# A hybrid block on one core: SSD decay taken off GpSimd, TensorE in program order there, and four smaller edits

## The chip, the cores and the metric

The kernel runs on one core of one Trainium2 chip. A core has five engines with an instruction queue each: TensorE (PE in the profile, PEld its weight loads), VectorE (DVE), ScalarE (ACT), GpSimd (POOL) and SyncE (SP), which here only issues DMAs. The metric is the time of one launch in microseconds; lower is better. Before the change it is 2102.24 us, the median of three runs from 2101.9 to 2103.63 us.

## The reference, cut to what matters

One layer on 256 tokens of width 2048, all in float32. The projection `w_in` of the normalised input feeds a stick-breaking attention, a Mamba-2 scan (SSD) and two gates; both mixers are merged, projected, normed and added to x; a gated MLP of width 5632 with a width-3 convolution follows, again normed and added. The part that the change touches most is the SSD, per group g of 8 heads (8 groups, head width 64, state 128), after a width-4 causal convolution and SiLU:

```
la = dt * a;  cs = cumsum(la)                       # falls along the tokens
decay = exp(where(causal, cs[l] - cs[s], -inf))     # per head, l >= s
cb    = C @ B^T                                     # per group
y     = (cb * decay) @ (x * dt)  +  carried state  +  x * d_skip
y     = rms_norm(y * silu(z), per group) 
```

## The kernel before, in words

**Weights.** All matrices stream from memory in 714 units of 128x1024 float32 (512 KB). SP issues the loads (L78). Each unit is split into a rounded half `whi` (a cast on ACT, L63) and a remainder `wlo` (a subtraction on DVE, L64). Five buffers of each exist and units are split three ahead of use, so the cast of unit n+5 waits until TensorE has finished unit n. `feat_mm` gives a tile of 128 features by 256 tokens (16 k-steps of a 512-column product, L112, and a 256-column one, L113); `tok_mm` gives two tiles of 128 tokens by 512 features (L145 to L147, three products per tile and k-step). Their banks are four of the eight PSUM banks; the pool `paux` has the other four.

**Background work.** Small products are put between the large ones by generators in a list `bg`; `pump()` advances the oldest by one `yield`, and `drain()` runs the list empty. `tok_mm` pumps after every fourth k-step, that is after every two units. Outside of a few hand-ordered places (`manual_schedule`) the framework's scheduler fixes each engine's order before the run, by its own priorities, close to program order; each queue then runs strictly in that order.

**Group loop.** A group does four `ps_xs` tiles, two `ps_bc` tiles (convolution on DVE, `cva`, and SiLU on ACT, L318), then `ps_z`. During `ps_z` and the next group's `ps_xs`, `ssd_work` (L323 to L380) runs in steps: transposes `px` of the convolved x (L332) with the scaled copies `xw` and `xd`; the decay matrix `mm` (csb minus cs_tok on DVE, L338; masked on GpSimd by `affine_select`, L339; exponential on ACT, L347; times `pcb` on DVE, L350); `pcb`, the C-by-B product (L343, L344), one pump after `px`; `po`, the carried-state product (L353), one pump later; `pd`, the decay product (L363), in two pumps; then gate, norm and the transposes `pt` (L385). `csb` is a broadcast of cs from a DRAM copy (L429).

**Around it.** At the start, ten pairs of products on `ones` keep TensorE busy (`wake`) while x chunk 0 and the first weights land. Between the mixers' output product `ps_mo` and the MLP's first tiles `ps_f` stands the norm `n1`: the block is scaled (L632), transposed (`pth`, L385) and split into halves `h` (L63, L64). After the last product `ps_fo` come the norm `n3` and the output: a sum of squares on ACT (L571), a product with the gain (L701), three small Newton steps (L594 to L596), nine multiply-adds (L726) and nine DMAs (L727) issued in turn by ACT and SP.

Of the kernel before, what the change touches and what calls it, by code (L numbers as in the profile page):

```python
# [29 lines left out]
C_N = KT + C_FB + 88  # L30

LNEXP = "natural_log_exp_and_others"
ACT_DVE = {mybir.EngineType.Activation, mybir.EngineType.DVE}
# [5 lines left out]
def block_kernel(ctx, tc, xT, xN, wts, vecs, rows, hvec, dskip, gain, out):  # L39
# [95 lines left out]

    def tok_mm(acts, nk, name):

        pss = [mm_bank(f"{name}_{t}") for t in range(2)]
        for k in range(nk):
            if k % 2 == 0:  # L140
                hi, lo = unit()
            w = slice(k % 2 * 512, k % 2 * 512 + 512)
            for t in range(2):
                ah, al = (acts[k // 4][:, k % 4, s, t * P:(t + 1) * P] for s in range(2))
                nc.tensor.matmul(pss[t], ah, hi[:, w], start=(k == 0), stop=False)  # L145
                nc.tensor.matmul(pss[t], ah, lo[:, w], start=False, stop=False)  # L146
                nc.tensor.matmul(pss[t], al, hi[:, w], start=False, stop=(k == nk - 1))  # L147
            if k % 4 == 3:
                pump()
        return pss  # L150
# [19 lines left out]
    for i in range(10):  # L170
# [152 lines left out]
    def ssd_work(g, xf, bf, cf, xs, csb):  # L323
        h8 = slice(8 * g, 8 * g + 8)
        sz, xd = xs[:, 0], xs[:, 1]
# [3 lines left out]
        for t in range(2):  # L329
# [4 lines left out]
            nc.scalar.copy(xd[:, t, :], px)  # L334
            nc.gpsimd.tensor_tensor(v3(xd[:, t, :]), v3(xd[:, t, :]), bc_in(dsk[:, h8], 64), op=ALU.mult)
        nc.gpsimd.tensor_tensor(v3(xw[:, 2, :]), v3(xw[:, 0, :]), bc_in(dec0[:, h8], 64), op=ALU.mult)
        for t in range(2):
            nc.vector.tensor_tensor(mm[:, t, :, :], csb[:, :, t * P:(t + 1) * P], bc_in(cs_tok[:, t, h8], P), op=ALU.subtract)  # L338
# [470 lines left out]
```

## Time and profile before

| | before |
|---|---|
| runs, median (range) | 2102.24 us (2101.9 to 2103.63) |
| the profiled execution | 2101.31 us, its span 2099.6 us |
| mean granted TensorE clock | 0.995 |
| TensorE busy | 2072.1 us, 99% |
| VectorE, ScalarE, GpSimd busy | 1386.0, 1156.9, 152.3 us |
| memory traffic | 191 GB/s over the span |

The profiled execution's own time is 1.71 us more than its span. A row of the timeline gives the start, the length, the engine, the line, the operation with its result and operands, how many instructions the row joins, and in brackets the idle time before it and what ended that. Matmuls overlap: successive 512-column products start about 0.23 us apart although each is listed with 0.39 us, so distances between starts, not lengths, say how long TensorE takes.

### The profile page before, as it was taken

To read this page: it belongs to the slowest core of one execution; us is meant where nothing else is said; L and a number is where in the kernel's file an instruction comes from. 1 tells how busy PE (TensorE), PEld (TensorE's weight loads), DVE (VectorE), ACT (ScalarE), POOL (GpSimd) and SP (SyncE) were. 2 spreads that over 40 slices of the span, in tenths; PEclk is the share of its full clock that TensorE was granted. 3 is DMA by queue.
4 is the path that set the end of the run, shared out by engine and by line. 5 is a ranking of instruction groups with operands and counts; after the bars stand their busy time and mean duration, and the time that the engine had idled before them with its cause. 6 is when DMAs were issued, how large, how long until landed. Compare 5 with 4: busy or idle time off the path is not lost.

```text
span 2099.6 us, 27950 instructions
## 1 busy us (share of the span) xinstructions
PE 2072.1 (99%) x10632; PEld 1760.7 (84%) x10632; DVE 1386.0 (66%) x1794; ACT 1156.9 (55%) x1542; POOL 152.3 (7%) x134
## 2 busy tenths in 40 slices
PE   9999999999999999999999999999999999999997
PEld 7788888888888888888888888788888888888886
DVE  6888877788544445555544566598878887854443
ACT  6767677667543334555556444475555555544442
POOL 0222102222000000000000021100000000000000
PEclk9999999999999999999999999999999999999999
DMA  8564565555555555555555746475555555565653
GB/s 297 194 205 160 190 205 186 176 199 179 187 197 192 192 194 186 180 171 171 170 172 185 274 161 210 141 250 191 189 190 190 189 189 190 191 232 202 195 193 109
DMA packets 109094, 402.79 MB, mean 192 GB/s; under 512 B 12416, under 2 KB 12672, under 8 KB 106656
## 3 DMA queue, kind: packets, MB, share of 16 engines
q1 hardware_dynamic: 104912, 380.07, 54.1%
q0 software_dynamic: 3328, 20.02, 2.7%
q8 instruction: 83, 1.36, 0.3%
q10 hardware_dynamic: 720, 0.93, 0.1%
q14 instruction: 51, 0.42, 0.1%
HBM read 396.71 MB, written 4.26 MB: 191 GB/s over the span
## 4 chain that ended last, share of the span: by engine, by line
PE 92%; POOL 2%; DVE 2%; issue 2%; DMA 1%; ACT 1%; SPq 0%; DVEq 0%; ACTq 0%; POOLq 0%
PE ps_fv L112 8%; PE ps_fg L112 8%; PE ps_qk L112 6%; PE ps_xs L112 5%; PE ps_fo L147 4%; PE ps_fo L145 4%; PE ps_fo L146 4%; PE ps_fg L113 4%; PE ps_fv L113 4%; PE ps_qk L113 3%; PE ps_ssd L147 3%; PE ps_ssd L145 3%; PE ps_ssd L146 3%; PE ps_xs L113 2%; PE ps_bc L112 2%; PE ps_z L146 2%
## 5 line engine op out<-in xcount | busy, mean ns | idle before, releaser
L64 DVE TENSOR_TENSOR wlo<-raw,whi 128x1024 fp32r<-128x1024 f32 (+1 forms) x715 | 905.1, 1270 | 601.2 <-ACT whi L63 600.6
L63 ACT CAST whi<-raw 128x1024 fp32r<-128x1024 f32 (+1 forms) x715 | 746.2, 1051 | 793.7 <-PE ps_fo L147 128.9
L112 PE MATMUL ps_fg<-h,whi 128*128 128x512 f32 x688 | 240.7, 394 | 0.0
L112 PE MATMUL ps_fv<-h,whi 128*128 128x512 f32 x688 | 240.6, 394 | 0.0
L113 PE MATMUL ps_fg<-h,wlo 128*128 128x256 f32 x688 | 190.6, 277 | 0.0
L113 PE MATMUL ps_fv<-h,wlo 128*128 128x256 f32 x688 | 190.6, 277 | 0.0
L112 PE MATMUL ps_qk<-a,whi 128*128 128x512 f32 x512 | 181.3, 398 | 0.0
L112 PE MATMUL ps_xs<-a,whi 128*128 128x512 f32 x464 | 162.9, 396 | 0.0
L112 PEld LDWEIGHTS ps_fv<-h,whi 128*128 128x128 f32 x688 | 129.0, 188 | 30.0
L112 PEld LDWEIGHTS ps_fg<-h,whi 128*128 128x128 f32 x688 | 129.0, 188 | 30.0
L113 PE MATMUL ps_qk<-a,wlo 128*128 128x256 f32 x512 | 143.5, 280 | 0.0
L145 PE MATMUL ps_fo<-whi,f 128*128 128x512 f32 x352 | 136.9, 389 | 0.0
L147 PE MATMUL ps_fo<-whi,f 128*128 128x512 f32 x352 | 136.9, 389 | 0.0
L146 PE MATMUL ps_fo<-wlo,f 128*128 128x512 f32 x352 | 136.9, 389 | 0.0
L113 PEld LDWEIGHTS ps_fg<-h,wlo 128*128 128x128 f32 x688 | 129.2, 188 | 0.0
L113 PEld LDWEIGHTS ps_fv<-h,wlo 128*128 128x128 f32 x688 | 129.2, 188 | 0.0
L113 PE MATMUL ps_xs<-a,wlo 128*128 128x256 f32 x464 | 129.0, 278 | 0.0
L112 PEld LDWEIGHTS ps_qk<-a,whi 128*128 128x128 f32 x512 | 96.1, 188 | 22.6
L145 PE MATMUL ps_z<-whi,a 128*128 128x512 f32 x256 | 103.7, 407 | 0.0
L112 PEld LDWEIGHTS ps_xs<-a,whi 128*128 128x128 f32 x464 | 87.1, 188 | 19.6
L146 PE MATMUL ps_z<-wlo,a 128*128 128x512 f32 x256 | 100.4, 392 | 1.0 <-DVE wlo L64 1.0
L147 PE MATMUL ps_z<-whi,a 128*128 128x512 f32 x256 | 100.1, 391 | 0.0
(282 smaller groups left out, 3832.5 us busy)
## 6 DMA issues: line engine op xcount, KB each, us to landing
raw<-wts SPq DMA_DIRECT2D x713, 512.0 KB, 3.8
csb<-cs_dram POOLq DMA_DIRECT2D x8, 1024.0 KB, 8.1
xt<-xN SPq DMA_DIRECT2D x2, 1024.0 KB, 10.6
csb<-gain POOLq DMA_DIRECT2D x8, 256.0 KB, 4.1
xn<-xN POOLq DMA_DIRECT2D x2, 1024.0 KB, 7.9
x_dram<-xn POOLq DMA_DIRECT2D x2, 1024.0 KB, 9.0
xe<-x_dram POOLq DMA_DIRECT2D x2, 1024.0 KB, 10.3
x<-xT SPq DMA_DIRECT2D x3, 512.0 KB, 9.2
```

What stands on the lines that cost most here:

```text
L63: nc.scalar.copy(hi, src)
L64: nc.vector.tensor_tensor(lo, src, hi.bitcast(F32), op=ALU.subtract)
L112: nc.tensor.matmul(ps, hi[:, w], act[:, k % 4, :, :].rearrange("p s t -> p (s t)"), start=(k == 0), stop=last)
L113: nc.tensor.matmul(ps[:, :T], lo[:, w], act[:, k % 4, 0, :], start=False, stop=last, skip_group_check=True)
L145: nc.tensor.matmul(pss[t], ah, hi[:, w], start=(k == 0), stop=False)
L146: nc.tensor.matmul(pss[t], ah, lo[:, w], start=False, stop=False)
L147: nc.tensor.matmul(pss[t], al, hi[:, w], start=False, stop=(k == nk - 1))
```

## The change

- **Decay and skip.** GpSimd loses all arithmetic of `ssd_work`. The skip product and the state-decay product go to DVE; the copy of `px` on ACT is gone, since DVE reads `px` in PSUM directly. The causal mask moves from `mm` (2048 columns, GpSimd) to `pcb` (two 128-column products with `m_le` on DVE, into `xw[:, 3]`), and the exponent is clamped by a Relu on ACT: per token tile one Relu and one Exp of 1024 columns in place of one Exp of 2048.
- **Order.** From group 1 to the end of the last group's work TensorE keeps program order. `csb`'s DMA is issued inside `ssd_work`. The `yield` between `px` and `pcb` is gone; `pd` and what follows come one pump later from group 1 on.
- **Loads.** The skip factors come with the vector load `vecs` in place of a DMA of their own. x chunk 0 is one DMA, not two halves, and `wake` has 12 pairs.
- **Small products.** `lead=True` puts one 64-column product on `ones` ahead of three tiles: `ps_qk0_0_0`, `ps_fg2`, `ps_fg3`.
- **n1.** The scalings, transposes and splits are written in another order.
- **Tail.** In the last `ps_fo` the final three units are first used for token tile 0 alone, then for tile 1; norm, scaling and output run tile by tile.

```diff
-    def feat_mm(acts, name):
+    def feat_mm(acts, name, lead=False):
         ps = mm_bank(name)
+        if lead:
+            nc.tensor.matmul(ps[:, :64], ones, ones[:, :64], start=True, stop=True)
...
+    def tok_mm_lag(acts, nk, name, lag=3):
+        pss = [mm_bank(f"{name}_{t}") for t in range(2)]
+        held = []
+        for k in range(nk):
+            left = (nk - 1 - k) // 2
+            if k % 2 == 0:
+                w = unit(min(WBUFS - 2, left) if left < lag else WBUFS - 2)
+            if left < lag:
+                held.append((k, w))
+                tok_step(pss, acts, k, nk, 0, *w)
+            else:
+                for t in range(2):
+                    tok_step(pss, acts, k, nk, t, *w)
+        for k, w in held:
+            tok_step(pss, acts, k, nk, 1, *w)
+        return pss
...
-    for i in range(10):
+    for i in range(12):
         nc.tensor.matmul(wake[:, :P], ones, ones, start=True, stop=True)
...
+    nc.sync.dma_start(x_raw[0], xT[:, 0:4, :])
     for i in range(2):
-        nc.sync.dma_start(x_raw[0][:, 2 * i:2 * i + 2, :], xT[:, 2 * i:2 * i + 2, :])
         nc.sync.dma_start(raw0[:, i * 512:i * 512 + 512], wts[0][:, i * 512:i * 512 + 512])
...
-    dsk = const.tile([P, 64], F32, name="dsk")
-    nc.gpsimd.dma_start(dsk, dskip.partition_broadcast(P))
+    dsk = vec[:, C_D:C_D + 64]
...
-    def ssd_work(g, xf, bf, cf, xs, csb):
+    def ssd_work(g, xf, bf, cf, xs):
+        csb = slot(F32, [8, T], f"csb{g}")
+        nc.gpsimd.dma_start(csb, cs_dram[h8, :].partition_broadcast(P))
+        if g > 0:
+            yield
...
-            nc.scalar.copy(xd[:, t, :], px)
-            nc.gpsimd.tensor_tensor(v3(xd[:, t, :]), v3(xd[:, t, :]), bc_in(dsk[:, h8], 64), op=ALU.mult)
-        nc.gpsimd.tensor_tensor(v3(xw[:, 2, :]), v3(xw[:, 0, :]), bc_in(dec0[:, h8], 64), op=ALU.mult)
-        for t in range(2):
-            nc.vector.tensor_tensor(mm[:, t, :, :], csb[:, :, t * P:(t + 1) * P], bc_in(cs_tok[:, t, h8], P), op=ALU.subtract)
-            nc.gpsimd.affine_select(out=mm[:, t, :, :], in_=mm[:, t, :, :], pattern=[[0, 8], [1, P]], compare_op=ALU.is_ge,
-                                    fill=-30000.0, base=0, channel_multiplier=-1)
-        yield
+            nc.vector.tensor_tensor(v3(xd[:, t, :]), v3(px), bc_in(dsk[:, h8], 64), op=ALU.mult)
         pcb = paux.tile([P, 512], F32, tag="aux", name=f"pcb{g}")
...
+        cbm = xw[:, 3, P:3 * P]
         nc.scalar.copy(xw[:, 3, 0:P], pcb[:, P:T])
+        for t in range(2):
+            nc.vector.tensor_tensor(cbm[:, t * P:(t + 1) * P], pcb[:, 256 * t:256 * t + P], m_le, op=ALU.mult)
         lnexp()
-        nc.scalar.activation(mm, mm, AF.Exp)
+        for t in range(2):
+            m = mm[:, t, :, :]
+            nc.vector.tensor_tensor(m, csb[:, :, t * P:(t + 1) * P], bc_in(cs_tok[:, t, h8], P), op=ALU.subtract)
+            nc.scalar.activation(m, m, AF.Relu, scale=-1.0)
+            nc.scalar.activation(m, m, AF.Exp, scale=-1.0)
+        nc.vector.tensor_tensor(v3(xw[:, 2, :]), v3(xw[:, 0, :]), bc_in(dec0[:, h8], 64), op=ALU.mult)
+        yield
...
-        nc.gpsimd.tensor_tensor(xd[:, 1, :], xd[:, 1, :], off, op=ALU.add)
+        nc.vector.tensor_tensor(xd[:, 1, :], xd[:, 1, :], off, op=ALU.add)
         yield
+        if g > 0:
+            yield
...
+        if g == 1:
+            order.enter_context(tc.manual_schedule(engines=PE))
...
+        for i in range(3):
+            scaled(i)
+        halves(0)
+        for i in range(3, 8):
+            halves(i - 2)
+            scaled(i)
+        halves(6)
+        halves(7)
...
-        n3.add(3, 0, ps[0])
-        n3.add(3, 1, ps[1])
-        gained(3, 0, gfo)
-        n3.last()
-        gained(3, 1, gfo)
-        n3.newton()
-        for n in range(4):
-            for t in range(2):
+        for t in range(2):
+            w = slice(t, t + 1)
+            n3.add(3, t, ps[t])
+            gained(3, t, gfo)
+            n3.last(w)
+            n3.newton(w)
+            for n in range(4):
```

How the order of the instructions moves is shown at three places. A row has the line, the operation, and result and operands; the number in a name is the tile's or the unit's, the last one a buffer's.

**Group 2, TensorE, around `px`.** First before, then with the change (`whi55` to `whi58` are weight units of `ps_z2`).

```order
L147 MATMUL ps_z2_1_1801<-whi55_1744,a0_117 128x512
L332 MATMUL px2_0_1840<-ident_203,xf2_0_1419 128x128
...
L332 MATMUL px2_1_1848<-ident_203,xf2_3_1614 128x128
L145 MATMUL ps_z2_0_1800<-whi56_1766,a1_136 128x512
...
L343 MATMUL pcb2_1901<-bc2_1_1786,bc2_0_1730 128x256
L344 MATMUL pcb2_1901<-bc2_1_1786,bc2_0_1730 128x128
L145 MATMUL ps_z2_0_1800<-whi58_1822,a2_153 128x512
```

```order
L146 MATMUL ps_z2_1_1796<-whi55_1739,a0_118 128x512
L362 MATMUL px2_0_1835<-ident_202,xf2_0_1404 128x128
...
L362 MATMUL px2_1_1842<-ident_202,xf2_3_1609 128x128
L366 MATMUL pcb2_1849<-bc2_1_1781,bc2_0_1710 128x256
L367 MATMUL pcb2_1849<-bc2_1_1781,bc2_0_1710 128x128
L144 MATMUL ps_z2_0_1795<-whi56_1761,a1_137 128x512
```

`pcb2` moved from behind unit 57 to directly behind `px2`, ahead of unit 56; its operand `bc2_1` is the SiLU of the group's last tile.

**The same place on ScalarE,** before and with the change: who writes `bc2_1`, and what stands around it.

```order
L315 ACTIVATE cva42_1790<-cvr42_1787,vec_93 128x256
L63 CAST whi60_1885<-raw60_1883 128x1024
L318 ACTIVATE bc2_1_1786<-cva42_1790 128x256
L334 COPY xs2_1799<-px2_0_1840 128x512
L334 COPY xs2_1799<-px2_1_1848 128x512
L63 CAST whi61_1911<-raw61_1909 128x1024
L347 ACTIVATE mm2_1839<-mm2_1839 128x2048
L345 COPY xw2_1838<-pcb2_1901 128x128
```

```order
L340 ACTIVATE cva42_1785<-cvr42_1782,vec_95 128x256
L65 CAST whi60_1883<-raw60_1881 128x1024
L343 ACTIVATE bc2_1_1781<-cva42_1785 128x256
L369 COPY xw2_1833<-pcb2_1849 128x128
L65 CAST whi61_1903<-raw61_1901 128x1024
L376 ACTIVATE mm2_1834<-mm2_1834 128x1024 x2
L377 ACTIVATE mm2_1834<-mm2_1834 128x1024 x2
```

The cast of unit 60 stands between the convolution's first step `cva42` and the SiLU `bc2_1` in both; the copy `xw2` from `pcb2`, which `po2` reads, moved from behind the exponential to directly behind the SiLU.

**Group 0, TensorE, around the decay product `pd0`** (units 22 and 23 are the first tile of group 1, unit 24 the second), before and with the change.

```order
L112 MATMUL ps_xs1_1_907<-a0_117,whi24_812 128x512
L363 MATMUL pd0_0_828<-xw0_680,mm0_681 128x64 x8
L113 MATMUL ps_xs1_1_907<-a0_117,wlo24_813 128x256
L112 MATMUL ps_xs1_1_907<-a0_117,whi24_812 128x512
L363 MATMUL pd0_1_896<-xw0_680,mm0_681 128x64 x8
```

```order
L114 MATMUL ps_xs1_0_839<-a2_154,whi23_790 128x512
L115 MATMUL ps_xs1_0_839<-a2_154,wlo23_791 128x256
L397 MATMUL pd0_0_824<-xw0_679,mm0_680 128x64 x8
L114 MATMUL ps_xs1_0_839<-a2_154,whi23_790 128x512
...
L115 MATMUL ps_xs1_0_839<-a3_173,wlo23_791 128x256
L397 MATMUL pd0_1_894<-xw0_679,mm0_680 128x64 x8
L114 MATMUL ps_xs1_1_905<-a0_118,whi24_808 128x512
```

`pd0_0` moved ahead by almost one unit, from inside unit 24 to behind the first k-step of unit 23, and `pd0_1` to the end of unit 23.

**n1, TensorE, up to the MLP's first product,** before and with the change.

```order
L385 MATMUL pth1_0_11080<-ident_203,mog0_10412 128x128 x4
L385 MATMUL pth1_1_11086<-ident_203,mog1_10413 128x128 x4
L385 MATMUL pth2_0_11094<-ident_203,mog0_10412 128x128 x4
L112 MATMUL ps_f0_0_11186<-h0_11049,whi450_10997 128x512
L113 MATMUL ps_f0_0_11186<-h0_11049,wlo450_10998 128x256
```

```order
L419 MATMUL pth0_1_11053<-ident_202,mog1_10392 128x128 x4
L419 MATMUL pth1_0_11059<-ident_202,mog0_10391 128x128 x4
L114 MATMUL ps_f0_0_11165<-h0_11028,whi450_10976 128x512
L115 MATMUL ps_f0_0_11165<-h0_11028,wlo450_10977 128x256
L114 MATMUL ps_f0_0_11165<-h0_11028,whi450_10976 128x512
```

Three transposed blocks stand ahead of the first `ps_f` product, not five; the other five stand between the products of units 450 and 451.

More of the change, by code (lines that the diff above doesn't have):

```diff
@@ L141, in tok_mm @@
                 hi, lo = unit()
[L142 removed]
             for t in range(2):
[L144 to L147, printed above, removed]
+                tok_step(pss, acts, k, nk, t, hi, lo)
             if k % 4 == 3:
                 pump()
+        return pss
[14 more added lines that the diff above has]
+            tok_step(pss, acts, k, nk, 1, *w)
         return pss
```

68 lines of the change are left out of this document (39 added, 29 removed).

## The prediction

> **What bounds the kernel now.** I read the page's busy times and chain first, then what TensorE waits for, then one stretch of a group.
>
> ```profile
> PE 2072.1 (99%) x10632; PEld 1760.7 (84%) x10632; DVE 1386.0 (66%) x1794; ACT 1156.9 (55%) x1542; POOL 152.3 (7%) x134
> PE 92%; POOL 2%; DVE 2%; issue 2%; DMA 1%; ACT 1%; SPq 0%; DVEq 0%; ACTq 0%; POOLq 0%
> PE po L353 <- ACT xw L345: 3.7, 6, 0.7
> PE pth L385 <- DVE mog L632: 2.9, 1, 2.9
> PE ps_first L112 <- DVE a L197: 2.9, 2, 2.1
> PE po L353 <- POOL xw L336: 2.4, 1, 2.4
> PE ps_z L146 <- DVE wlo L64: 1.0, 1, 1.0
> 125.45:188.30 62.85, 62.75 (x345) 53.73 (x345) 50.69 (x68) 44.54 (x60) 12.22 (x8) 1.00 0.57 194
> 188.30:251.15 62.85, 62.25 (x343) 53.32 (x342) 51.19 (x71) 44.74 (x60) 12.22 (x8) 1.00 0.56 188
> ```
>
> TensorE sets the time. The waits (total, times, longest) and the tail are all there is to win without taking products away: po 6.1 us, n1 2.9, start 2.9, one unit 1.0. The last two rows are two group periods with the busy time of PE, PEld, DVE, ACT, POOL: DVE has 12 us to spare, ACT 18. So work that moves to them is free, and what counts is where TensorE, in its fixed order, meets a result that isn't there yet.
>
> **The groups: pcb becomes a wait (+7.6).** The change puts `pcb` directly behind `px`. Its operand is the SiLU of the last tile. In group 2:
>
> ```profile
> 188.57 1.04 PE L332 MATMUL px<-ident,xf 128*128 128x128 f32 x8
> 188.27 1.52 DVE L317 SCALAR_TENSOR_TENSOR cva<-cvr,vec,cva 128x255 f32<-128x255 f32 x3
> 188.77 1.05 ACT L63 CAST whi<-raw 128x1024 fp32r<-128x1024 f32 x1 [1.18 <-PE ps_z L147]
> 189.36 0.48 PE L145 MATMUL ps_z<-whi,a 128*128 128x512 f32 x1
> 189.88 0.42 ACT L318 ACTIVATE bc<-cva 128x256 f32<-128x256 f32 x1
> 201.40 0.24 ACT L345 COPY xw<-pcb 128x128 f32<-128x128 f32 x1
> 201.79 1.10 PE L353 MATMUL po<-xw 128*128 128x512 f32 x2 [0.60 <-ACT xw L345]
> 125.23 0.42 ACT L318 ACTIVATE bc<-cva 128x256 f32<-128x256 f32 x1 [0.51 <-DVE cva L317]
> ```
>
> TensorE is through with `px` at 189.36. The SiLU ends at 190.30, and from the end of an ACT result to TensorE's start the `po` row shows 0.15 (201.64 to 201.79). So `pcb` starts at 190.45, 1.09 late. Before, it stood 5.5 us further on and never waited. Nothing in the change brings the SiLU forward: ahead of it on ACT stands the cast of unit 60, which waits for the last product of unit 55, the one ahead of `px`; and DVE's three convolution steps end at 189.79 anyway. Both chains hang on TensorE's own progress, so the stall returns each period. Group 1 had the SiLU ahead of that cast (125.65, `px` later); with the change its order is the same as in the others. Seven groups: +7.6. Bounds: 0, if the SiLU is as early in all as it was in group 1; 8.4, at 1.2 each, if the wait costs one more handoff. I take 7.6, since six of seven groups show the rows above.
>
> **The groups: po stops waiting (-3.0).** Before, the copy of `pcb` stood behind the 1.92 us exponential, that behind GpSimd's mask; now directly behind the SiLU, 10 us ahead of `po`. The windows put the price at 62.75 - 62.25 = 0.50 us of PE per group in six groups. Bounds -3.7 (the row of waits) and -1.5.
>
> **The groups: DVE's load (0).** GpSimd's rows lie beside slow DVE rows:
>
> ```profile
> 80.32 2.36 DVE L338 TENSOR_TENSOR mm<-csb,cs_tok 128x1024 f32<-128x1024 f32 x2 [3.63 <-DMA csb<-cs_dram]
> 190.90 3.68 DVE L338 TENSOR_TENSOR mm<-csb,cs_tok 128x1024 f32<-128x1024 f32 x2
> 191.49 4.00 POOL L335 TENSOR_TENSOR xs<-xs,dsk 128x512 f32<-128x512 f32 x2
> 194.50 4.09 DVE L64 TENSOR_TENSOR wlo<-raw,whi 128x1024 fp32r<-128x1024 f32 x2
> 204.04 2.36 DVE L64 TENSOR_TENSOR wlo<-raw,whi 128x1024 fp32r<-128x1024 f32 x2
> ```
>
> The same two subtractions take 2.36 with GpSimd idle and 3.68 beside it, two `wlo` 2.36 and 4.09: 3.05 us per group that DVE gets back. It gains two 128x512 products from PSUM (about 0.65 each by `xw`'s kind), two 128-column masks (0.3), two more 128x512 (0.65): some 3.2 us. DVE stands as before, with 12 us of slack in a period: 0. Without that cover a late `wlo` would stop TensorE as it does once before (1.0). The Trainium skill, "SBUF — State Buffer", section "SBUF: two separate sides", says that VectorE and GpSimd share one port pair as an exclusive lock; by the full lock DVE would win the whole 8 us of the two GpSimd rows, by the rows it wins 3.05, and the measurement decides. As TensorE doesn't wait for DVE there, either sum gives 0.
>
> **Group 0 (+0.7).** Here the scheduler orders.
>
> ```profile
> 77.64 1.13 PE L353 MATMUL po<-xw 128*128 128x512 f32 x2 [2.39 <-POOL xw L336]
> 82.51 0.39 PE L112 MATMUL ps_xs<-a,whi 128*128 128x512 f32 x1
> 85.69 1.92 ACT L347 ACTIVATE mm<-mm 128x2048 f32<-128x2048 f32 x1 [1.33 <-POOL mm L339]
> 89.01 1.97 PE L363 MATMUL pd<-xw,mm 128*128 128x64 f32 x16
> 91.22 1.89 PE L363 MATMUL pd<-xw,mm 128*128 128x64 f32 x16
> ```
>
> The wait of `po` for GpSimd, 2.39, goes. But `csb` still lands at 80.3, and `pd0_0` now stands behind unit 22 and one k-step, where TensorE arrives at 82.51 - 2.39 + 2.83 + 0.35 = 83.3 (a unit is 8 pairs at 0.353). The first subtraction ends at 81.5, and behind it come two Relus and the first Exp, at half of 1.92 and a handoff each, to about 84.7; ahead of the product with `pcb` DVE has `wlo24`, the `po` step and `wlo25` (1.2, 0.7, 1.2): `pd0_0` at about 86.85, 3.5 us late. Then 1.70, seven pairs (2.47) and 1.70: unit 24 starts at 92.7. Before, unit 24 and both `pd` together cost the same work by about 92.0. So +0.7; -2.4 if that wait doesn't come, +1.5 if both `wlo` are late.
>
> **Start (-0.3).**
>
> ```profile
> 9.95 0.79 PE L112 MATMUL ps_first<-a,whi 128*128 128x512 f32 x1 [2.13 <-DVE a L197]
> 58.73 0.50 PE L146 MATMUL ps_z<-wlo,a 128*128 128x512 f32 x1 [1.00 <-DVE wlo L64]
> ```
>
> One DMA for x chunk 0 brings its second half earlier, the first later. Up to 1.5 us of the 2.13 may go; but at 58.73 TensorE waits 1.0 for DVE, busy with a chain that begins with x's own load, and that doesn't move. So most is given back there. Bounds -1.5 and +0.3.
>
> **n1 (+1.25).**
>
> ```profile
> 1352.10 2.74 DVE L632 SCALAR_TENSOR_TENSOR mog<-mog,n_r,xg 128x512 f32<-128x512 f32 x4
> 1353.00 4.21 PE L385 MATMUL pth<-ident,mog 128*128 128x128 f32 x20 [2.91 <-DVE mog L632]
> 1356.01 0.68 DVE L64 TENSOR_TENSOR h<-pth,h 128x512 fp32r<-128x512 f32 x1
> 1356.97 0.48 PE L112 MATMUL ps_f<-h,whi 128*128 128x512 f32 x1
> 1363.57 3.38 DVE L64 TENSOR_TENSOR wlo<-raw,whi 128x1024 fp32r<-128x1024 f32 x2 [1.23 <-ACT whi L63]
> 1366.88 4.05 DVE L647 SCALAR_TENSOR_TENSOR xn<-mo,n_r,xn 128x512 f32<-128x512 f32 x6
> 1370.86 2.35 DVE L64 TENSOR_TENSOR wlo<-raw,whi 128x1024 fp32r<-128x1024 f32 x2
> ```
>
> With three scalings ahead, not four, the second split moves up and `ps_f` starts some 0.7 earlier, but two of the five transposes (0.4 each) come after it: +0.1. DVE's first splits now wait for ACT's casts, its eight scalings and eight splits end about 0.7 later, ACT's casts too. The first `wlo` of the last row (unit 455) lands at 1372.04; TensorE needs it five units (2.83 each) and three transposes (0.4 each) after 1356.97, at 1372.3. Some 0.7 later for the scalings and splits and 0.6 for the casts behind them, it is about 1.1 late. Sum +1.25; -0.3 with the splits on time, +3.5 if TensorE's pause keeps it slow (below).
>
> **Small products (+0.6).** A `pd` issue is 16 records in 1.70 us (89.01 row), 0.106 each, and a 64-column product is two: 0.2 each for three; no wait stands there that they could fill. Bounds 0 and 0.7.
>
> **Tail (-1.0).**
>
> ```profile
> 2086.49 0.39 PE L147 MATMUL ps_fo<-whi,f 128*128 128x512 f32 x1
> 2086.91 0.60 ACT L571 ACTIVATE n_j<-ps_fo 128x512 f32<-128x512 f32 x1
> 2088.89 5.52 DVE L726 SCALAR_TENSOR_TENSOR fo<-fo,n_r,xe 128x512 f32<-128x512 f32 x9
> 2089.68 4.71 ACTq L727 DMA_DIRECT2D out_dram<-fo  x4
> ```
>
> Call the last product's start M (2086.49). Tile 0 ends 18 products (4.1 us) earlier, so by the same steps its four multiply-adds run from M-1.0 to M+1.6. Tile 1's square sum on ACT could start at M+0.42 as before, but it stands behind two DMA issues of tile 0, the second of which waits for the third multiply-add: M+1.1, plus 0.34 of issue. From M+1.45 the chain of 2086.91 to 2088.89, with the gain product now in it, ends at M+4.1; five multiply-adds (2.9) end at M+7.0, before at M+7.92. So -1.0; -2.2 if ACT doesn't wait on its issues, -0.4 if the output DMAs bunch.
>
> **Sum.** 7.6 - 3.0 + 0.7 - 0.3 + 1.25 + 0.6 - 1.0 = +5.85. On the profiled execution, 2101.31: 2107.2. The median of the runs shown, 2102.24, lies 0.93 higher: 2108.1. I take 2107.5.
>
> **Rivals.** *No pcb wait.* For it: group 1's SiLU, early before. Against: six groups and the order on ACT. Without the term: 2107.5 - 7.6 = 2099.9, no change. *Half of it,* if TensorE's stall lets ACT and DVE run ahead once and stay there: 2103.7, no change. Against: the cast waits for the product ahead of `px`, whatever came before. *Faster:* no pcb wait, and tail and start at their good ends (-1.2 each): 2097.5; this decides if the SiLU ends within 0.2 us of `px`. *Slower clock:* behind the 2.91 us pause at n1, 20 transpose records take 4.0 us, 0.20 each, against 0.10 for `px` (8 in 0.79); now TensorE idles some 0.8 us more between transposes and `ps_f`, and if it stays at half speed for five pairs of 0.353, 1.8 us go: 2109.3. The Trainium skill, "TensorE: Matmul & The Clock Gate", Part 1, has the clock at half after an idle window of about 3.4 us and full after a busy one, with windows that run freely; by it this varies from run to run. The trace agrees in kind (0.20 against 0.10).
>
> **Numbers.** Forecast 0.48, slower clock 0.09, half 0.17, no pcb wait 0.12, faster 0.14. A measurement here tells about 0.2% (4.2 us) from none. Of the forecast 0.07 lies within it: slower 0.50, same 0.07 + 0.17 + 0.12 = 0.36, faster 0.14. The range, 2097.5 to 2110.5, takes in the rivals but half of the faster one; the forecast's own is 2105 to 2110.
>
> **What would show it.** In the waits of TensorE a row `pcb` <- ACT `bc`, 7 times, near 1.1, and no `po` row; right if the group period is 62.85 + 0.6. `pd` waiting once, near 87. At n1, `ps_f` at 0.7 sooner after `ps_mo` and a `wlo` wait near 14 us later. At the end the last multiply-add at M+7. I am wrong if no `pcb` row appears, or if TensorE waits in the groups for a `wlo`.

## The result and the profile after

The changed kernel takes 2116.64 us, the median of four runs (2114.5 to 2120.1), against 2102.07 for the kernel before in the same session (2100.75 to 2103.63): a ratio of 1.0071, with a 95% interval of 1.0053 to 1.0088. It is slower, as forecast, but by 14.6 us and not by 5.4, and it lies above the range. The profiled execution took 2114.5 us with a span of 2112.8, which is 13.2 more than the span before. The working below splits these 13.2 us.

First TensorE's busy time on the page of the changed kernel, and its waits (total, times, longest):

```profile
PE 2083.4 (99%) x10642; PEld 1766.2 (84%) x10642; DVE 1379.9 (65%) x1846; ACT 1158.5 (55%) x1547; POOL 63.2 (3%) x85
PE pcb L366 <- ACT bc L343: 8.4, 7, 2.2
PE pth L419 <- DVE mog L671: 2.9, 1, 2.9
PE pd L397 <- DVE mm L382: 1.5, 1, 1.5
PE ps_z L145 <- DVE wlo L66: 1.2, 1, 1.2
PE rx_ps L278 <- DVE rx_dg L277: 1.0, 1, 1.0
```

The forecast row is there: `pcb` waits seven times for the SiLU, and no `po` row is left; `pth` waits as before. But TensorE's *busy* time also grew, by 11.3 us (2072.1 before), with ten products more. A busy time that grows without work is the first sign of the step that the prediction lacked.

To see where the offset arises, the starts of the same products in both traces were set side by side. The differences add up to the span's 13.2:

| stretch | grows by, us | predicted |
|---|---|---|
| start to the first `ps_z` | -2.80 | -0.3 |
| group 0 | +0.85 | +0.7 |
| groups 1 to 7, to `ps_ssd` | +6.95 | +4.6 |
| `ps_qk0` to the end of `ps_mo` | -0.64 | +0.2 |
| n1, to the first `ps_fg` | +1.22 | +1.25 |
| MLP, first `ps_fg` to `ps_fo` | +9.66 | +0.4 |
| `ps_fo` | 0.0 | 0 |
| tail | -2.08 | -1.0 |

**The MLP.** This is the large error. The groups of instructions of the kernel before, and then of the changed one, for the same 688 products (total, mean in ns):

```profile
L112 PE MATMUL ps_fg<-h,whi 128*128 128x512 f32 x688 | 240.7, 394 | 0.0
L112 PE MATMUL ps_qk<-a,whi 128*128 128x512 f32 x512 | 181.3, 398 | 0.0
```

```profile
L114 PE MATMUL ps_fg<-h,whi 128*128 128x512 f32 x688 | 245.2, 399 | 0.0
```

The products are the same and wait for nothing, but a `ps_fg` product is listed with 399 ns, not 394 (`ps_fv` with 398 or 399, and 394 before). The timeline of TensorE in the changed kernel shows the place where that begins, the small product ahead of `ps_fg3`, and where the MLP ends:

```profile
1398.08 0.39 PE L114 MATMUL ps_fv<-h,whi 128*128 128x512 f32 x1
1398.43 0.39 PE L114 MATMUL ps_fv<-h,whi 128*128 128x512 f32 x1
1398.78 0.33 PE L121 MATMUL ps_fg<-ones 128*128 128x64 f32 x2
1398.92 0.48 PE L114 MATMUL ps_fg<-h,whi 128*128 128x512 f32 x1
...
1399.35 0.40 PE L114 MATMUL ps_fg<-h,whi 128*128 128x512 f32 x1
1399.70 0.40 PE L114 MATMUL ps_fg<-h,whi 128*128 128x512 f32 x1
...
1862.57 0.40 PE L144 MATMUL ps_fo<-whi,f 128*128 128x512 f32 x1
```

The same two products in the kernel before:

```profile
1392.50 0.39 PE L112 MATMUL ps_fg<-h,whi 128*128 128x512 f32 x1
...
1847.33 0.39 PE L145 MATMUL ps_fo<-whi,f 128*128 128x512 f32 x1
```

A pair (a 512- and a 256-column product) starts every 0.347 us ahead of the small product and every 0.353 us behind it, to the end of the MLP. Between the first `ps_fg3` product and `ps_fo` stand 82 tiles of 16 pairs: (1862.57 - 1398.92) / 82 = 5.654 us a tile, before (1847.33 - 1392.50) / 82 = 5.547, and 82 times the difference is 8.8 of the 9.66 us. I call these the *short* and the *long* rhythm. Both stand in the trace of before too: its `ps_qk` row has 398 ns beside 394 for `ps_fg`. In the MLP a switch is seen only behind a small product, a product of another tile that stands out of turn, or a wait. It isn't the clock: a window of the MLP in the changed kernel, and then one of before, have the granted clock at 1.00, with fewer products (2617, 2622) in more time:

```profile
1400.00:1862.00 462.00, 462.00 (x2617) 400.62 (x2616) 366.89 (x576) 260.03 (x410) 1.07 (x2) 1.00 0.57 189
```

```profile
1393.00:1847.00 454.00, 454.00 (x2622) 397.02 (x2621) 368.46 (x582) 261.94 (x413) 1.07 (x2) 1.00 0.59 192
```

**The groups.** Group 1 lost far more than the others. In the changed kernel, DVE, ACT and TensorE there, then TensorE's same wait in group 2:

```profile
124.39 0.48 DVE L342 SCALAR_TENSOR_TENSOR cva<-cvr,vec,cva 128x255 f32<-128x255 f32 x1
124.87 0.69 DVE L363 TENSOR_TENSOR xw<-px,dt_tok 128x512 f32<-128x512 f32 x1
125.48 0.47 DVE L342 SCALAR_TENSOR_TENSOR cva<-cvr,vec,cva 128x254 f32<-128x254 f32 x1
125.87 0.68 DVE L364 TENSOR_TENSOR xs<-px,vec 128x512 f32<-128x512 f32 x1
126.47 0.47 DVE L342 SCALAR_TENSOR_TENSOR cva<-cvr,vec,cva 128x253 f32<-128x253 f32 x1
127.04 0.42 ACT L343 ACTIVATE bc<-cva 128x256 f32<-128x256 f32 x1 [1.56 <-DVE cva L342]
127.51 0.70 PE L366 MATMUL pcb<-bc,bc 128*128 128x256 f32 x2 [2.24 <-ACT bc L343]
...
192.51 0.70 PE L366 MATMUL pcb<-bc,bc 128*128 128x256 f32 x2 [1.02 <-ACT bc L343]
```

Two products on `px` (`xw`, which was on DVE before too, and `xs`, which came to it) stand between the three convolution steps on which the SiLU waits; in group 2 the three steps run without a break. So the wait is 2.24 us and not 1.02. What follows it shows in the windows of the changed kernel (length, busy time of PE, PEld, DVE, ACT, POOL, then the granted clock as a share of full speed, DMA share, GB/s):

```profile
118.76:128.00 9.24, 7.00 (x36) 5.72 (x35) 9.23 (x15) 4.75 (x7) 0.00 (x0) 1.00 0.86 281
128.00:132.00 4.00, 4.00 (x13) 3.19 (x13) 4.00 (x7) 3.47 (x4) 0.90 (x2) 0.57 0.02 6
132.00:136.00 4.00, 4.00 (x19) 3.29 (x18) 3.56 (x4) 3.50 (x5) 0.19 (x1) 1.00 0.77 180
```

TensorE is busy for 7.00 of the first 9.24 us, the rest is the wait. From 128.3 to 131.7 the clock is at half and products start 0.43 us apart, not 0.23; 13 products fit where otherwise 19 do. That takes another 1.7 us. The Trainium skill, "TensorE: Matmul & The Clock Gate", Part 1, has the clock at half after at least one idle window of about 3.4 us; here the half clock lasted such a time (3.4), but an idle time of 2.24 was enough, so in this the measurement corrects the page.

**The tail.** The last product starts at M = 2101.73 here. In the timeline of the changed kernel:

```profile
2100.64 2.74 DVE L774 SCALAR_TENSOR_TENSOR fo<-fo,n_r,xe 128x512 f32<-128x512 f32 x4
2103.14 0.60 ACT L609 ACTIVATE n_j<-ps_fo 128x512 f32<-128x512 f32 x1 [3.11 <-DVE fo L774]
2105.70 2.87 DVE L774 SCALAR_TENSOR_TENSOR fo<-fo,n_r,xe 128x512 f32<-128x512 f32 x5
```

Tile 1's square sum stands behind tile 0's output issues, as the prediction had it (M+1.41, forecast M+1.45), and the last multiply-add ends at 2108.57, M+6.84. The span then ends at M+11.03, 4.2 after it; before it was 5.2.

### The profile page after: what moved, and what is told of

It is laid out like the page before. It is cut to its first block, busy times and chain, and to the rows that moved or that the text cites. A ratio compares the mean times of both kernels' runs of the same rounds, so it can differ in the third digit from the quotient of the medians.

```text
span 2112.8 us, 27918 instructions
## 1 busy us (share of the span) xinstructions
PE 2083.4 (99%) x10642; PEld 1766.2 (84%) x10642; DVE 1379.9 (65%) x1846; ACT 1158.5 (55%) x1547; POOL 63.2 (3%) x85
## 4 chain that ended last, share of the span: by engine, by line
PE 92%; DVE 3%; DMA 2%; ACT 1%; issue 1%; SPq 0%; DVEq 0%; ACTq 0%
PE ps_fv L114 8%; PE ps_fg L114 8%; PE ps_qk L114 6%; PE ps_xs L114 5%; PE ps_fv L115 4%; PE ps_fg L115 4%; PE ps_fo L145 4%; PE ps_fo L144 4%; PE ps_fo L146 4%; PE ps_qk L115 3%; PE ps_ssd L144 3%; PE ps_ssd L146 3%; PE ps_ssd L145 3%; PE ps_xs L115 2%; PE ps_z L145 2%; PE ps_z L146 2%
## 5 line engine op out<-in xcount | busy, mean ns | idle before, releaser
L66 DVE TENSOR_TENSOR wlo<-raw,whi 128x1024 fp32r<-128x1024 f32 (+1 forms) x715 | 884.6, 1241 | 639.1 <-ACT whi L65 637.9
L114 PE MATMUL ps_fg<-h,whi 128*128 128x512 f32 x688 | 245.2, 399 | 0.0
L114 PE MATMUL ps_fv<-h,whi 128*128 128x512 f32 x688 | 244.9, 398 | 0.0
```

The source lines that it names most:

```text
L66: nc.vector.tensor_tensor(lo, src, hi.bitcast(F32), op=ALU.subtract)
L114: nc.tensor.matmul(ps, hi[:, w], act[:, k % 4, :, :].rearrange("p s t -> p (s t)"), start=(k == 0), stop=last)
```

## The experiments

Three things were to be told apart. *What `pcb` costs:* by the theory the seven waits and the half clock are one cause that goes when `pcb` is issued a pump later; by its rival the groups are slow because of DVE's new load and stay so. *What sets the MLP's rhythm:* the product ahead of `ps_fg3` by itself, or n1's new order (which puts the broadcast product `r_ps` of the norm n2, a 256-column one, inside tile `ps_fg2` where it stood ahead of that tile), or small products at tile seams in some other combination. *What the tail is worth alone.* The mean of the `ps_fv` rows (394 or 398 to 399 ns) serves as the mark of the rhythm in the profiled execution.

### pcb one pump later

The changed kernel, with the `yield` ahead of `pcb` back from group 1 on:

```diff
+        if g > 0:
+            yield
         pcb = paux.tile([P, 512], F32, tag="aux", name=f"pcb{g}")
...
-        yield
+        if g == 0:
+            yield
```

> The changed kernel with pcb one pump (24 products) later again in groups 1 to 7, everything else as changed. Theory (pcb's wait for the SiLU is lost time): no pcb row among TensorE's waits, which held 8.4 us, po without a wait, so 8.4 us less in the groups and 2116.6 - 8.4 = 2108.2 if the MLP keeps its rhythm. Rival (the stall gives others time that they need, so the wait moves to po or a weight unit): at most 3 us less, 2113.6 or above, with a new row of waits in the groups.

Measured: 2106.14 us (2102.54 to 2107.93, ten runs), 1.0017 (1.0007 to 1.0028); 10.5 us less than the changed kernel. No `pcb` and no `po` row is left among the waits, and the clock of group 1 stays full (1.00 from 128 to 132 us). A window of one group period of this kernel (columns as above):

```profile
189.60:251.71 62.11, 62.11 (x344) 53.45 (x343) 49.99 (x77) 44.30 (x60) 1.08 (x2) 1.00 0.58 190
```

The MLP of this kernel keeps the long rhythm; what it shows is the groups. TensorE is busy for all of the 62.11 us, while DVE carries 50 us in it: DVE's load is not what holds the groups. The period is 0.74 shorter than before the change and 1.29 shorter than with the `pcb` wait (63.40). So both terms of the prediction were too small, and by nearly the same: `po` and what goes with it is worth 0.74 a group, not 0.50, and a `pcb` stall costs 1.29, of which the wait itself is 1.02. Their difference, 0.55, is what it said (0.59).

### The product ahead of ps_fg3: none, or two

Two kernels, the changed one without that product, and with two of them:

```diff
-        pg = feat_mm(h_ch, f"ps_fg{j}", lead=j in (2, 3))
+        pg = feat_mm(h_ch, f"ps_fg{j}", lead=j == 2)
```
```diff
-        if lead:
+        for _ in range(lead):
...
+        pg = feat_mm(h_ch, f"ps_fg{j}", lead={2: 1, 3: 2}.get(j, 0))
```

> The changed kernel without the small product ahead of ps_fg3 alone; the one ahead of ps_fg2 stays. Theory A (two rhythms: from that product on, all 82 later MLP tiles run at 5.653 us instead of 5.547): the tiles go back to 5.547, the time falls by 82 x 0.107 + 0.2 = 9.0 us, to about 2107.6 from 2116.6, and the span to about 2103.8. Rival B (the MLP is slow for another reason, such as the moved small product r2_ps, the late unit 455 or a slower clock): the tiles stay at 5.65 and the time falls by 0.2 us.

> The changed kernel with two small products ahead of ps_fg3 in place of one. Theory A1 (each small product turns the rhythm over): two turn it twice, the tiles run at 5.547 and the time is 9 - 0.4 = 8.5 us below the changed kernel, about 2108. Theory A2 (any small product at that place leaves the slow rhythm behind): the tiles stay at 5.653, the time at 2116.8. Rival B (the MLP is slow for another reason): 2116.8.

Without it: 2108.62 us (2104.53 to 2114.13, seven runs), 1.0035 (1.0024 to 1.0046). With two: 2109.11 (2103.96 to 2109.6, six runs), 1.0024 (1.0011 to 1.0037). Groups of the one without, then of the one with two:

```profile
L114 PE MATMUL ps_fv<-h,whi 128*128 128x512 f32 x688 | 245.1, 399 | 0.0
```

```profile
L114 PE MATMUL ps_fv<-h,whi 128*128 128x512 f32 x688 | 240.6, 394 | 0.0
```

Two products left the short rhythm in place, one did not: the rhythm depends on the small products. But without it, the profiled run (2114.13) has the long rhythm as well. It begins earlier there, inside the tile `ps_fg1`, where a `ps_fv` product stands out of turn and TensorE then waits 0.19 us for a `wlo`, and neither the product ahead of `ps_fg2` nor `r_ps`, inside that tile in this kernel, ends it. Its other times reach down to 2104.5. So the product ahead of `ps_fg3` isn't the only way in.

### The same product in the kernel before

```diff
-        pg = feat_mm(h_ch, f"ps_fg{j}")
+        pg = feat_mm(h_ch, f"ps_fg{j}", lead=j == 3)
```

> The kernel before with nothing added but the small product ahead of ps_fg3. Theory A: the rhythm of the 82 later MLP tiles turns from 5.547 to 5.653, so 2102.1 + 9.0 = 2111 us. Rival B (the product costs its own 0.2 us, the MLP is slow for another reason): 2102.3.

Measured: 2101.99 us (2100.35 to 2103.22, ten runs), 1.0002 (0.9993 to 1.0011). Its groups:

```profile
L112 PE MATMUL ps_fv<-h,whi 128*128 128x512 f32 x688 | 240.6, 394 | 0.0
```

Here the same product in the same place does nothing. The theory that it switches the rhythm by itself fell.

### n1's new order alone in the kernel before

```diff
-        lag = 3
-        for i in range(8 + lag):
...
+        for i in range(3):
+            scaled(i)
+        halves(0)
+        for i in range(3, 8):
+            halves(i - 2)
+            scaled(i)
```

> The kernel before with the changed order at n1 and nothing else; r2_ps then stands four k-steps into ps_fg2, no longer at the seam ahead of it. Theory 1 (n1 itself costs 1.2 us by the late unit 455; the rhythm depends on the disturbance and its place): 2101.8 + 1.2 = 2103.0 if the MLP stays fast, and 2111.7 with tiles at 5.653 if r2_ps inside the tile leaves the slow rhythm. Rival (slow MLP tiles come from the small products alone): 2103.0, tiles at 5.547.

Measured: 2110.95 us (2103.95 to 2114.94, ten runs), 1.0038 (1.0026 to 1.005). The ten times lie in two heaps, three from 2104 to 2106 and seven from 2109.9 to 2115. In the profiled execution (2114.94) the rhythm is long. Its groups, and TensorE's timeline inside `ps_fg1` and around `r_ps`:

```profile
L112 PE MATMUL ps_fv<-h,whi 128*128 128x512 f32 x688 | 245.1, 399 | 0.0
```

```profile
1376.71 0.40 PE L112 MATMUL ps_fv<-h,whi 128*128 128x512 f32 x1
1377.30 0.38 PE L113 MATMUL ps_fg<-h,wlo 128*128 128x256 f32 x1 [0.20 <-DVE wlo L64]
...
1386.78 0.67 PE L253 MATMUL r_ps<-r_dg,ones 128*128 128x256 f32 x2
1387.10 0.58 PE L112 MATMUL ps_fg<-h,whi 128*128 128x512 f32 x1
```

In the kernel before, `r_ps` stands at the seam of the two tiles:

```profile
1380.86 0.28 PE L113 MATMUL ps_fv<-h,wlo 128*128 128x256 f32 x1
1380.97 0.60 PE L253 MATMUL r_ps<-r_dg,ones 128*128 128x256 f32 x2
```

So n1's order alone can cost as much as the small products. It does two things: a `ps_fv` product comes to stand inside `ps_fg1`, and `r_ps` moves a few products into its tile. In this execution the pairs start 0.347 us apart ahead of the first place and 0.353 behind it, and `r_ps` leaves them so; in the kernel before they are at 0.353 up to `r_ps`, and `r_ps` at the seam makes them short. Five more executions have n1's new order, all with a small product ahead of `ps_fg2`: from ahead of that product to behind `r_ps` the rhythm stays short in the changed kernel, turns long with `pcb` later, stays long without the product ahead of `ps_fg3`, and turns short with two of them and in the changed kernel with several sizes (below). From the first `ps_f` product to `r_ps` TensorE runs the same 157 products in the same order in all five, so the order alone doesn't decide.

### Two products alone, and the products without n1's order

The kernel before with products ahead of `ps_fg2` and `ps_fg3` only; and the changed kernel with n1 as it was:

```diff
-        pg = feat_mm(h_ch, f"ps_fg{j}")
+        pg = feat_mm(h_ch, f"ps_fg{j}", lead=(64,) if j in (2, 3) else ())
```
```diff
-        for i in range(3):
-            scaled(i)
-        halves(0)
...
+        lag = 3
+        for i in range(8 + lag):
```

> The kernel before with the small products ahead of ps_fg2 and ps_fg3 and nothing else of the change; the first stands directly behind r2_ps. Theory E (the two products together leave the slow rhythm, whatever the rest of the kernel is): tiles at 5.653 us from ps_fg2 or ps_fg3 on, 2101.5 + 0.4 + 8.9 = 2110.8 us. Rival (only in the changed kernel, as the one ahead of ps_fg3 alone left the kernel before fast): tiles at 5.547, 2101.9.

> The changed kernel with n1 in the order of the kernel before, all else as changed, the small products too; r2_ps then stands at the seam ahead of ps_fg2. Theory (the order at n1 is what slows the MLP, by its own 1.2 us and by the rhythm): 2116.6 - 8.7 - 1.2 = 2106.7, tiles at 5.547. Rival (the small product ahead of ps_fg3 slows it in the changed kernel whatever n1 does): 2115.4, tiles at 5.653.

The two products alone: 2111.3 us (2110.73 to 2111.99, four runs), 1.0045 (1.0031 to 1.0059), 9.6 above the kernel before in that session. Without n1's order: 2116.51 (2114.96 to 2116.71, four runs), 1.0067 (1.0054 to 1.008), no gain. Groups and timeline of the kernel with the two products alone:

```profile
L112 PE MATMUL ps_fv<-h,whi 128*128 128x512 f32 x688 | 245.0, 399 | 0.0
```

```profile
1381.48 0.59 PE L255 MATMUL r_ps<-r_dg,ones 128*128 128x256 f32 x2
1381.91 0.33 PE L118 MATMUL ps_fg<-ones 128*128 128x64 f32 x2
```

Here `r_ps` stands at the seam, where alone it leaves the short rhythm, but a 64-column product follows directly, and from `ps_fg2` on the rhythm is long; the one ahead of `ps_fg3` leaves it so. This settles the cost: two products of 64 columns, which the prediction put at 0.2 us each, take 9.6 us. The products are enough by themselves, and n1's order is in seven of ten runs; taking one away alone doesn't help reliably. The changed kernel with n1's order and no small product in the MLP was not run.

### Small products of several sizes

Three kernels, run once each, to find which product switches the rhythm. In the first two, of the kernel before and of the changed one, tiles from `ps_fg4` on get in turn 32 columns, 64, none, 128, and twice 64; in the third, of the kernel before, mostly one of 64:

```diff
+        pg = feat_mm(h_ch, f"ps_fg{j}", lead=() if j < 4 else ((64,), (), (128,), (64, 64), (32,))[j % 5])
```
```diff
+        pg = feat_mm(h_ch, f"ps_fg{j}", lead=(64,) if j == 2 or 4 <= j < 20 or j > 24 else (64, 64) if j == 20 else (32,) if j == 22 else ())
```

> The kernel before with products on ones ahead of the gate tiles from ps_fg4 on, of five kinds in turn: one of 64 columns, none, one of 128, two of 64, one of 32. Theory A1 (each product turns the rhythm over): the rhythm turns at each single product, not at none and not at two. Theory A3 (a product sets the rhythm anew, by how long it takes and the phase it meets): turns at some kinds only, the same kind always with the same result from the same rhythm. Rival B (products have nothing to do with the rhythm): no turn anywhere.

> The changed kernel with the same five kinds of products on ones ahead of the gate tiles from ps_fg4 on as in the run e7_lead_mix, which had them in the kernel before and in which two of 64 columns always left the slow rhythm, one of 64 always the fast, and one of 32 kept what it met. Theory C (what a product does at a seam of tiles depends on what it is, not on the kernel): the same pattern here, so one of 64 ahead of ps_fg6 and every fifth gate tile after it gives 5.547. Rival D (what it does depends on where in its cycle TensorE's order of products was left by r2_ps, two products into a pair and inside a tile): other results for the same kinds, one of 64 leaving the slow rhythm as it did ahead of ps_fg3.

> The kernel before with one product of 64 columns ahead of ps_fg2 and of every gate tile from ps_fg4 to ps_fg19, two ahead of ps_fg20, one of 32 ahead of ps_fg22, and one of 64 ahead of every gate tile from ps_fg25 on. Theory F (one of 64 keeps a slow rhythm that comes from another one of 64, and makes it fast when it comes from one of 32): slow from ps_fg2 to ps_fg20, then slow behind the two, fast from ps_fg25 on. Theory G (one of 64 always ends fast where nothing else stands beside it): slow at most to ps_fg4, fast to ps_fg20, slow to ps_fg25, fast after. Rival H (each one of 64 turns the rhythm over): it alternates from gate tile to gate tile.

One time each: 2112.09, 2119.82 and 2117.69 us. What each product did, read from the distances between starts in the tile ahead of it and behind it:

| kernel | product | rhythm ahead and behind |
|---|---|---|
| before, in turn | 64 twice | short to long, 8 of 8 |
| | 32 | keeps it: long 7, short 1 |
| | 64, behind a tile with 32 | long to short 7, stays short 1 |
| | none; 128 | keeps it |
| changed, in turn | 64 ahead of `ps_fg3` | short to long |
| | from `ps_fg5` on | the same pattern as in the first kernel |
| before, mostly 64 | 64 sixteen times in a row | stays long |
| | 64 twice | long to short |
| | 32, then 64 nineteen times | stays short |

Within an execution the outcome repeats as the pattern of products repeats, but no rule by a product's size fits: one of 64 switched to long, switched to short, and left either as it was; two of 64 went both ways. What came earlier must count too. Of the rules expected for the third kernel none held throughout; the first, theory F, failed only at the two products ahead of `ps_fg20`, which left the short rhythm and not the long one.

### The tail alone

The kernel before with the changed last `ps_fo`, norm and output:

```diff
-        ps = tok_mm(f_ch, FF_T, f"ps_fo{n}")
+        ps = (tok_mm if n < 3 else tok_mm_lag)(f_ch, FF_T, f"ps_fo{n}")
...
+            n3.last(w)
+            n3.newton(w)
```

> The kernel before with the changed tail alone (the last three units of ps_fo by token tile, norm and output tile by tile). By the changed kernel's trace the end lies 2.04 us nearer to the last product than before, so 2101.8 - 2.0 = 2099.8. By the prediction, which counted the multiply-adds alone: 2100.8. Rival (the gain there came from a quieter memory queue that only the whole change has): 2101.8.

Measured: 2099.79 us (2097.76 to 2105.14, ten runs), 0.9989 (0.998 to 0.9998), 1.9 less by medians. It agrees with the -2.08 read from the traces (2.04 in the expectation, with spans rounded to 0.1), twice the -1.0 of the prediction.

### What is left when the costly parts are undone

First the changed kernel with `pcb` later, n1's old order and no products ahead of MLP tiles (the one ahead of `ps_qk0_0_0` stays); then, on top of it, group 0's `pd` a pump later; then, on the first, an output by tile with tile 0's DMAs all on SP and tile 1's norm ahead of tile 0's last multiply-add; last, both together.

```diff
-        pg = feat_mm(h_ch, f"ps_fg{j}", lead=j in (2, 3))
+        pg = feat_mm(h_ch, f"ps_fg{j}")
```
```diff
         yield
-        if g > 0:
-            yield
+        yield
```
```diff
+        for n in range(3):
+            put(n, 0)
+        n3.add(3, 1, ps[1])
+        gained(3, 1, gfo)
+        n3.last(slice(1, 2))
+        put(3, 0)
```

> The changed kernel with pcb one pump later (as in the run e4_pcb_later), n1 in the order of the kernel before and no small products in the MLP; the one ahead of ps_qk0_0_0 stays. Theory (the rhythm that the MLP has after its last disturbance lasts to its end, and here that disturbance is r2_ps at a seam of tiles, as before, where it left the fast rhythm): the tiles run at 5.547 us, 8.7 less in all; no small products 0.4 less; n1 as before 1.2 less. From the 2106.1 of e4_pcb_later that is 2095.8, ratio to before 0.997. Rival (the rhythm is drawn by chance in each run): a mixture of about 2096 and 2104.5.

> e5_best_guess with the decay products pd0 of group 0 one pump later, as in the other groups. Theory (their wait for mm, 1.5 us in e5_best_guess's trace, is lost time): no pd row among the waits, 1.5 us less, 2091.7. Rival (the time goes to the next thing that waits on VectorE in group 0, so nothing is won): 2093.2, with a new row of waits before 130 us.

> e5_best_guess with all output DMAs of token tile 0 issued by SP and tile 1's norm started ahead of tile 0's last multiply-add, so that ACT's square sum of tile 1 doesn't stand behind DMA issues. Theory (that wait, M+0.4 to M+1.4, sets the end): the square sum starts at M+0.4, the last multiply-add ends at M+5.8 in place of M+6.8, 1.0 us less, 2092.2. Rival (the end is set by the DMAs, whose issues now bunch on SP): 2093.2 or more.

> e11_g0_later with the tail of e12_tail_sp. By e12's trace the end lies 1.0 us nearer to the last product (last multiply-add at M+5.9, before M+6.85), which its times did not show because group 0 waited 1.8 us longer in them; here that wait is gone: 2089.0 - 1.0 = 2088.0, ratio 0.9935. Rival (the end is set by the DMAs): 2089.0.

| kernel | us, median (range), runs | ratio to before |
|---|---|---|
| costly parts undone | 2093.19 (2091.88 to 2095.35), 5 | 0.9957 (0.9944 to 0.9969) |
| and group 0's `pd` later | 2088.97 (2088.08 to 2089.47), 5 | 0.9937 (0.9925 to 0.9949) |
| and the output | 2093.77 (2089.22 to 2095.44), 6 | 0.9956 (0.9945 to 0.9968) |
| both | 2088.1 (2087.41 to 2088.6), 5 | 0.9934 (0.9921 to 0.9948) |

The groups of the first show the short rhythm, and three of TensorE's waits of the last show what remains:

```profile
L114 PE MATMUL ps_fv<-h,whi 128*128 128x512 f32 x688 | 240.6, 394 | 0.0
```

```profile
PE pth L421 <- DVE mog L674: 2.9, 1, 2.9
PE rx_ps L278 <- DVE rx_dg L277: 1.9, 1, 1.9
PE pd L399 <- DVE mm L385: 0.4, 1, 0.4
```

The last is faster than both kernels, by 13.6 and 28.5 us. Group 0's `pd` a pump later gave 4.2 us by medians, not the 1.5 of the wait it was to take away; in the profiled executions 2.4 of it lie in group 0 (67.48 us from `ps_z` to `ps_z` against 69.90) and 1.7 ahead of it. Much of both is the clock: without the later `pd` it was at half from 38.83 to 42.24 us, behind `rx_ps`'s wait of 1.8, and from 83.20 to 90.03, behind `pd`'s 1.5; with it, it stayed full, behind waits of 1.2 and 1.0. The first of the two has nothing to do with `pd`, so a part of the gain in these two executions is luck. The new output shortens the last step in the trace (last multiply-add at M+5.92, not M+6.85), but its interval can't be told from the kernel without it; in its profiled execution group 0's `pd` waited 3.3, which hides 0.9.

## Why the prediction was right or wrong

The sign was right and the mechanism in the groups as well; the size was wrong, and the one step that failed badly is "Small products (+0.6)". Of the other terms, the start was 2.5 us too high and the groups 2.5 too low; that these cancel is luck.

- **pcb becomes a wait (+7.6), po stops waiting (-3.0).** Right in kind, in place and in number: seven `pcb` waits for `bc`, none for `po`, 1.02 each in six groups (forecast 1.09), and a period 0.55 longer (0.59). The sizes of both were low (1.29 and 0.74, by the kernel with `pcb` later) and cancelled. Missed: group 1, taken to be like the others. There the products on `px` stand between DVE's convolution steps, the wait is 2.24, and the half clock behind it takes another 1.7 us. With this the stretch came to +6.95, not +4.6. The "slower clock" rival named the mechanism, but at n1. There the changed kernel has full clock again at 1360.50, ahead of `ps_f` at 1360.69; in the kernels without the product ahead of `ps_fg3` and with n1's order alone the first `ps_f` pairs do run at half clock (0.80 us apart), so the rival's case occurs, in some executions.
- **DVE's load (0).** Right as a sum: 1379.9 us against 1386.0, and no wait for a `wlo` in the groups. But where on DVE a product lands mattered in group 1, though the sum didn't. The 8 us by the full lock are no sound price: GpSimd's own rows are longer beside VectorE (2.02 us for an `xs` product that took 1.30 once), so they hold waiting of their own.
- **Group 0 (+0.7).** +0.85 in the profile, with the `pd` wait; the number is luck. The wait was 1.53 and not 3.5, and the working has no half clock, which follows the wait from 83.92 to 87.33 us (pairs 0.64 us apart, not 0.35) and takes another 1.7: -2.39 + 1.53 + 1.7 = 0.84. Both differ between the executions profiled: with two products ahead of `ps_fg3` the wait was 4.2 and the half clock lasted 6.8, and this group took 73.11 us, not 69.92.
- **Start (-0.3).** Wrong in size: -2.8. `ps_xs` starts 4.1 earlier, where the prediction had allowed 1.5 at most. It counted the wait of 2.13 alone, but from within that wait, at 8.69 us, to 15.52 the kernel before runs at half clock (granted 0.69 over 5 to 16 us), and the changed kernel, in which that wait is gone, doesn't (1.00). All seven profiled executions with the old start show such a half clock, of 3.4 or 6.8 us, and none of the ten with the new one. Of the 4.1, 1.3 is given back by the first `ps_z`, 1.04 of it in the new `rx_ps` wait. The `ps_z` wait, at which it would have given nearly all back, grew only from 1.00 to 1.24.
- **n1 (+1.25).** Right in time, +1.22: `ps_f` 0.63 sooner behind `ps_mo` (forecast 0.7), one `wlo` wait behind it. But the order also shifts `r_ps` into a tile and puts a `ps_fv` product inside `ps_fg1`, and alone it costs 9 us by medians in the kernel before. The working counted the stretch up to the first `ps_fg` and not what it hands on.
- **Small products (+0.6).** This failed. It priced them by the time they themselves take and held 0.7 to be the most. In the runs a small product can change the rhythm of all that follows: -0.64 behind the one ahead of `ps_qk0_0_0` (eight tiles go from 0.353 a pair to 0.347, more than it costs; read from the trace, not run alone), and 8.8 us in the MLP. The two MLP products alone measured 9.6. The trace of before had the cue: two means, 398 and 394 ns, for products of the same shape with nothing waiting, which I read past, since I worked with 0.353 a pair throughout.
- **Tail (-1.0).** The chain was right to 0.2 us (last multiply-add M+6.84, forecast M+7.0). The term missed that the output DMAs also land 1.0 sooner behind it, 4.2 against 5.2. Measured -2.08, and -1.9 alone.

By profile, the predicted +5.85 becomes +13.2 thus: start -2.5, groups and group 0 +2.5, small products +8.4, tail -1.08, n1 0.0. With the small products at their predicted price the kernel would have come out near +4.8, inside the forecast.

## What to carry to other kernels

Where TensorE is 99% busy, compare the mean length of the same product across stages of the profile before trusting one price per product: two means with no wait beside them are two rhythms, set by something that came before, and 2% of a long stage outweighs many single waits. Price an inserted product by what follows it, not only by its own length, and measure it alone: here one of 64 columns was followed by 0.6 us less (by the trace) or by no change, and two added 9.6. And before a dependent product is moved up, ask what its operand's engine will do just then; one pump of distance was worth 10.5 us. A wait can cost more than its length: look at the granted clock behind it.

## What the runs showed of the hardware

- Back-to-back 512- and 256-column pairs with an own weight load each run at 0.3467 or at 0.3533 us a pair, 1.9% apart, at a granted clock of 1.00 in both. In the MLP the rhythm lasts until a small product, a product out of turn or a wait, and can last 82 tiles. With the two products alone four runs lie within 1.3 us; with n1's new order the outcome differed from run to run, at the same order of products. What in TensorE chooses it is open: product size alone doesn't (the table above), and the weight loads' part in it was not tried.
- The granted clock falls to half behind some waits of TensorE and not behind others as long. In the changed kernel's trace it changes at 83.92, 87.33, 128.29, 131.70, 1357.09 and 1360.50 us; these lie 1, 12, 1, 359 and 1 times 3.413 us apart, so the changes keep to a grid. What counts by the traces is how long TensorE is idle between two neighbouring points of it. In all traces together, an interval at full clock with 2.0 us or more of idle time was always followed by half clock, one with less than 1.3 never, and those between sometimes. The grid lies elsewhere in each execution: group 0's `pd` wait of 1.53 in the changed kernel, all in one interval, was followed by half clock; group 0's `po` wait of 2.39 in the kernel before and n1's 2.91 in the kernel with the costly parts undone, each split over two intervals, were not. The rows are, in this order, two intervals of the changed kernel and its group 2 with the wait of 1.02, then two of the kernel before, then two of the kernel with the costly parts undone:

```profile
80.50:83.92 3.42, 1.89 (x18) 1.78 (x17) 3.26 (x4) 3.39 (x5) 0.00 (x0) 1.00 0.97 289
83.92:87.33 3.41, 3.41 (x13) 2.92 (x13) 2.97 (x4) 1.54 (x2) 0.00 (x0) 0.50 0.86 351
192.00:196.00 4.00, 3.49 (x16) 2.96 (x17) 4.00 (x8) 1.97 (x3) 0.00 (x0) 1.00 0.34 119
...
73.55:76.96 3.41, 1.70 (x8) 1.09 (x6) 3.01 (x2) 1.06 (x1) 3.41 (x3) 1.00 0.97 303
76.96:80.37 3.41, 2.73 (x10) 1.94 (x11) 0.05 (x1) 0.36 (x1) 0.63 (x1) 1.00 1.00 411
...
1342.72:1346.14 3.42, 1.54 (x7) 0.94 (x5) 1.74 (x6) 1.77 (x6) 0.00 (x0) 1.00 0.30 114
1346.14:1349.55 3.41, 2.28 (x16) 1.67 (x16) 3.37 (x7) 1.57 (x3) 0.00 (x0) 1.00 0.00 0
```

So in the changed kernel a wait of 2.24 us cost some 4 us where one of 1.02 cost 1.3.
